# A two-layer hybrid mixer step: the order of the projections in a layer, the filler's rate, and all elementwise work of GpSimd moved to VectorE and ScalarE

## The chip, the cores and the metric

The kernel runs on one core of a Trainium2 chip. The core has TensorE (PE in the profile, with its weight loads as PEld), VectorE (DVE), ScalarE (ACT), GpSimd (POOL) and SyncE (SP). SP and ACT issue the DMA transfers here. The metric is the device time of one execution in microseconds; before the change it is 2315.56 us, the median of three runs (2311.65 to 2316.22).

## The reference

One inference step of a backbone of two layers over 128 context tokens and 512 latent tokens, 640 rows in all, of width 2048. Each layer is one mixer:

```python
def layer_step(x, cvec, p, rope, attend, s0_f, s0_b):
    shift, scale, gate = adaln(cvec, w_ada, b_ada)     # silu(cvec) @ w_ada + b_ada
    h = rms_norm(x, norm_g) * (1.0 + scale) + shift
    aq, ak, av, ag, bq, bff, bfb, bi, bg, cu, cv, cg = split_proj(h @ w_in)
    q, k, v = qkv_heads(aq, ak, av, qg, kg, rope)
    a_out = attend(q, k, v) * jax.nn.silu(ag)
    b_out, s_f, s_b = hgrn_mixer(bq, bff, bfb, bi, bg, lb, hg, s0_f, s0_b)
    c_out = sgu_mixer(cu, cv, cg, lng, lnb, ws, bs)
    y = jnp.concatenate([a_out, b_out, c_out], axis=-1) @ w_out
    return x + gate * y, k, v, s_f, s_b
```

`attend` is windowed attention with 8 query heads and 2 key heads. `hgrn_mixer` is a gated linear recurrence in both directions with 4 heads. `sgu_mixer` normalises `cv`, mixes it over 128 positions in 4 groups and returns `cu * s * silu(cg)`. The forget gates of the recurrence have lower bounds from a softmax over the layers. The outputs are both activations, the new keys and values, and the final states of the recurrence. All is float32.

## The kernel before

**Projections.** Activations are kept transposed, 16 tiles of 128 x 640 per layer. Each float32 operand is split in two parts, `hh` and `hl` for the activations, `wh` and `wl` for the weights (lines 640 and 641: a copy on ACT and a subtraction on DVE), and three products of the parts are summed in PSUM. A projection is either row-major (`rowmajor`, line 663: 512 columns, 15 groups, five PSUM banks) or column-major (`colmajor`, line 680: 128 columns, 4 groups, two banks). There are five PSUM banks for projections and three for all else.

**Order of the work.** The program is written out in full by Python, and a planner places the instructions of each engine by its estimates and by priority, which is the order in which the program names them; the block `hi()` raises it. While a projection's matmuls are written, `tick()` takes one step of the first generator in the list `side` (attention, recurrence, spatial mix), 3 ticks per row-major group and 2 per column-major group, so that their small matmuls stand between the large ones. `flush()` takes all remaining steps at once.

**The filler.** After each group `fill()` (line 328) adds `fill_rate` to a credit and takes one step of the filler for each whole credit. The filler is `ada_steps` (line 290): it sums the modulation of a later use on DVE, one weight slice of 128 x 512 per step (two instructions, lines 300 and 302), 16 slices to a block, and then PE sums the accumulator over the partitions (lines 308 and 319). With two further steps a block has 18. The slices have two buffers and there is one accumulator `aacc`. Layer 0 has 12 blocks: four for its own gate, eight for layer 1's shift and scale. `drain()` takes all steps that are left. In layer 1 four more blocks run at rate 0.5.

**The first layer's start.** x arrives transposed. `first_norm` (line 360) squares it on ACT and sums it over the width on PE with a matrix of ones. `first_round` then computes the first modulation columns and the key projection. `setup` runs ahead of both, `setup2` after `second_round`.

**The rest of a layer.** After the queries and the BI projection (line 326), layer 0 computes CU 1 to 3 and CG 0 and parks them in DRAM (`cud`). Then come four heads of the recurrence (lines 334 to 340; each BFF, BFB, BQ and BG, and the generator `hgrn` of 35 steps joins `side`), the attention gates AG (line 343), CV with the spatial mix `sgu` (line 1164), the remaining AG, and CU and CG (layer 1) or CG 1 to 3 (layer 0). `mul_evac` (line 1202) reads a gate from PSUM, multiplies it into its place and applies the sigmoid; its last product is on POOL for AG and on DVE for CG. `split_mix` (line 1223) splits the 16 tiles of the mixer's output, a quarter of them on POOL, into buffers that the last projection frees one by one. `out_proj` (line 1236) multiplies by the gate and adds x, the addition on POOL for three quarters of the columns; the result of layer 0 is stored by SP. Layer 1 starts with `norm_x`, `scale_x` and `make_h` (line 603), where half of the `hl` are on POOL.

## Time and profile before

| what | us |
|---|---|
| median of 3 runs | 2315.56 |
| lowest and highest | 2311.65 and 2316.22 |
| the profiled execution's own time | 2315.77 |
| its span, first to last instruction | 2313.9 |
| PE busy | 2255.9 |
| DVE busy | 1391.7 |
| ACT busy | 894.0 |
| POOL busy | 120.6 |

The span is what the trace covers; 1.9 us of the execution's own time lie around it. Busy times are sums over one execution. An engine executes its instructions in order, so an instruction that waits holds all that stand behind it on that engine. A row of the profile names an instruction by its line in the kernel, its engine, its operation, and the tiles that it writes and reads (`out<-in`). A wait is put down to what came last before the instruction could start. The granted clock is the share of TensorE's full clock.

### The profile page before, as it was taken

What the parts mean: (1) busy time and instruction counts of PE and PEld (TensorE: products, weight loads), DVE (VectorE), ACT (ScalarE), POOL (GpSimd) and SP (SyncE); (2) the same over time, 40 slices, a digit from 0 to 9 for tenths busy, and PEclk for the clock granted to TensorE, in tenths of its full rate; (3) what the DMA queues carried; (4) which work ended last, traced back from release to release, by engine and by line L of the source; (5) the groups of instructions that cost most, each with busy time, mean ns of one, the idle gap of its engine ahead of it and who ended that gap; (6) DMA issues with size and microseconds to landing.
All of it is one profiled execution on the core that took longest, in us unless ns stands there. A gap on an engine that the chain in (4) does not pass through costs nothing.

```text
span 2313.9 us, 35246 instructions
## 1 busy us (share of the span) xinstructions
PE 2255.9 (97%) x13308; PEld 1958.9 (85%) x13308; DVE 1391.7 (60%) x2686; ACT 894.0 (39%) x2165; POOL 120.6 (5%) x82
## 2 busy tenths in 40 slices
PE   7999999999999999989999999999999999999999
PEld 5766678999999888977787888799999998998887
DVE  3435888877787757665667456855865932434222
ACT  4323334445456522322225234344565542223111
POOL 0000000000000101101112000000000000100110
PEclk9999999999999999999999999999999999999999
DMA  9675633534443445355552221422422423324332
GB/s 329 215 250 184 222 114 91 156 98 125 121 134 98 119 153 155 116 188 161 177 179 82 81 66 50 122 60 75 126 78 77 123 85 92 103 75 150 106 109 82
DMA packets 264878, 296.42 MB, mean 128 GB/s; under 512 B 17378, under 2 KB 166772, under 8 KB 262916
## 3 DMA queue, kind: packets, MB, share of 16 engines
q1 hardware_dynamic: 254368, 271.27, 37.9%
q10 hardware_dynamic: 10340, 22.91, 3.1%
q8 instruction: 104, 1.70, 0.3%
q14 instruction: 66, 0.54, 0.1%
HBM read 280.38 MB, written 13.73 MB: 127 GB/s over the span
## 4 chain that ended last, share of the span: by engine, by line
PE 53%; DVE 6%; DMA 3%; issue 1%; ACT 1%; DVEq 0%; ACTq 0%
PE m L660 21%; PE m L653 9%; PE m L652 9%; PE m L654 9%; DMA wa<-in_w_ada_dram 3%; DVE aacc L302 2%; DVE wl L641 1%; PE s L895 1%; PE s L941 1%; PE s L1108 1%; DVE ev L1261 0%; PE s L319 0%; PE s L1196 0%; PE s L953 0%; PE s L954 0%
## 5 line engine op out<-in xcount | busy, mean ns | idle before, releaser
L641 DVE TENSOR_TENSOR wl<-wr,wh 128x512 fp32r<-128x512 f32 (+1 forms) x535 | 386.9, 725 | 569.2 <-ACT wh L640 562.3
L640 ACT ACTIVATE wh<-wr 128x512 fp32r<-128x512 f32 (+1 forms) x535 | 336.1, 629 | 925.8 <-PE m L654 543.0
L652 PE MATMUL m<-wh,hh 128*128 128x512 f32 x1440 | 571.3, 397 | 9.7 <-DVE mg L1211 6.2
L653 PE MATMUL m<-wl,hh 128*128 128x512 f32 x1440 | 567.1, 394 | 3.5 <-DVE wl L641 3.3
L654 PE MATMUL m<-wh,hl 128*128 128x512 f32 x1440 | 564.9, 393 | 0.0
L660 PE MATMUL m<-hh,wh 128*128 128x384 f32 x2016 | 479.9, 317 | 0.0
L660 PE MATMUL m<-hl,wh 128*128 128x384 f32 x2016 | 465.1, 310 | 0.0
L660 PE MATMUL m<-hh,wl 128*128 128x384 f32 x2016 | 464.8, 310 | 0.0
L302 DVE SCALAR_TENSOR_TENSOR aacc<-wa,s,aacc 128x512 f32<-128x512 f32 x480 | 354.6, 770 | 76.9 <-DMA wa<-in_w_ada_dram 76.2
L652 PEld LDWEIGHTS m<-wh,hh 128*128 128x128 f32 x1440 | 271.9, 189 | 84.6 <-issue 10.3
L653 PEld LDWEIGHTS m<-wl,hh 128*128 128x128 f32 x1440 | 272.1, 189 | 64.2 <-DVE wl L641 7.1
L660 PEld LDWEIGHTS m<-hh,wh 128*128 128x128 f32 x2016 | 311.1, 189 | 13.6 <-issue 12.1
L654 PEld LDWEIGHTS m<-wh,hl 128*128 128x128 f32 x1440 | 271.9, 189 | 58.2 <-issue 2.2
L660 PEld LDWEIGHTS m<-hh,wl 128*128 128x128 f32 x2016 | 310.2, 189 | 1.8 <-issue 1.4
L660 PEld LDWEIGHTS m<-hl,wh 128*128 128x128 f32 x2016 | 310.4, 189 | 1.2 <-issue 0.8
L1094 ACT ACTIVATE mg<-ev,Dt 128x32 f32<-128x32 f32 x480 | 113.0, 309 | 9.4 <-PE s L1108 9.2
L1214 POOL TENSOR_TENSOR mg<-mg,ev 128x640 f32<-128x640 f32 x16 | 26.6, 1663 | 1513.8 <-ACT ev L229 1493.2
L925 ACT ACTIVATE g<-g,st,qs 128x384 f32<-128x384 f32 (+1 forms) x64 | 48.1, 752 | 36.3 <-DVE st L921 36.3
L1263 POOL TENSOR_TENSOR mg<-mg,ev 128x512 f32<-128x512 f32 x30 | 44.4, 1491 | 286.2 <-DVE ev L1261 285.4
L944 ACT ACTIVATE g<-s 128x512 fp32r<-128x512 f32 x56 | 32.5, 596 | 57.5 <-PE s L941 54.1
L945 DVE TENSOR_TENSOR g<-s,g 128x512 fp32r<-128x512 f32 x56 | 38.4, 688 | 23.4 <-ACT g L944 17.0
L1111 DVE COPY_PREDICATED att<-m,s 128x128 f32<-128x128 uint8 x80 | 22.8, 301 | 39.8 <-PE s L1108 39.0
(274 smaller groups left out, 1930.6 us busy)
## 6 DMA issues: line engine op xcount, KB each, us to landing
wr<-in_w_in_dram SPq DMA_DIRECT2D x406, 256.0 KB, 2.9
wa<-in_w_ada_dram SPq DMA_DIRECT2D x278, 256.0 KB, 2.9
wr<-in_w_out_dram SPq DMA_DIRECT2D x128, 256.0 KB, 2.9
wa<-in_w_ada_dram SPq DMA_DIRECT2D x16, 1024.0 KB, 5.3
wa<-in_w_in_dram SPq DMA_DIRECT2D x9, 1024.0 KB, 6.3
wa<-in_w_ada_dram SPq DMA_DIRECT2D x44, 128.0 KB, 3.4
mg<-const_xT_dram SPq DMA_DIRECT2D x4, 1280.0 KB, 5.9
x<-mg SPq DMA_DIRECT2D x20, 256.0 KB, 2.5
```

Source lines behind the costliest of these rows:

```text
L302: nc.vector.scalar_tensor_tensor(acc[:, cd], r, sc, acc[:, cd], op0=ALU.mult, op1=ALU.add)
L640: nc.scalar.activation(wh, raw, AF.Copy)
L641: nc.vector.tensor_tensor(wl, raw, wh.bitcast(F32), op=ALU.subtract)
L652: nc.tensor.matmul(ps, lhsT=hh, rhs=wh[:, 0], start=k == 0, stop=False)
L653: nc.tensor.matmul(ps, lhsT=hh, rhs=wl[:, 0], start=False, stop=False)
L654: nc.tensor.matmul(ps, lhsT=hl, rhs=wh[:, 0], start=False, stop=k == KT - 1)
L660: self.nc.tensor.matmul(ps[hf][:, 0:n], lhsT=w[:, a], rhs=h[:, o:o + n], start=k == 0 and i == 0, stop=k == KT - 1 and i == 2)
L925: nc.scalar.activation(dst[h], src[h], AF.Exp, bias=nmx[:, h:h + 1], scale=rq[:, h:h + 1], accum_out=den[:, h:h + 1])
L944: nc.scalar.activation(pt[0], pb, AF.Copy)
L945: nc.vector.tensor_tensor(pt[1], pb, pt[0].bitcast(F32), op=ALU.subtract)
L1094: nc.scalar.activation(blk[:, 4 * i + q], e[:, q], AF.Copy, scale=dd[:, i, c:c + 1])
L1263: (nc.vector if c == 3 else nc.gpsimd).tensor_tensor(xs, xs, y, op=ALU.add)
```

## The change

1. `first_norm`: the squares are added up on DVE, and PE multiplies the one sum with the matrix of ones (2 products stay of 32).
2. The softmax of the forget bounds (12 operations on DVE, one Exp on ACT) moves from `setup` to the beginning of `setup2`.
3. The division of the attention weights moves from DVE to ACT, and so does the copy of the recurrence's output from PSUM.
4. All of POOL's elementwise work moves to DVE: the `hl` in `make_h` and `split_mix`, the products of the norm in `sgu`, the last product in `mul_evac`, the additions of `out_proj`.
5. The order in a layer: pairs of CU and CG (`cgate`), multiplied and parked in DRAM, three of them ahead of the recurrence's heads in layer 0 and one in layer 1, the others after a head each. Five AG heads follow, then CV, then AG 5 to 7 while the spatial mix runs; these evacuate at once, with another pool of buffers for the sigmoid. After the flush the parked products are loaded and multiplied in, now in both layers.
6. The spatial mix waits ten steps for its matmuls where it waited six.
7. The filler's rate in layer 0 is 0.85 where it was 1.0, and 1.25 in the out-projection.

```diff
     def setup2(self):
...
@@ first_norm
+        tot = self.g()
         for k in range(KT):
-            s = self.g()
+            s = self.g() if k else tot
             nc.scalar.activation(s, xm[k // 4][:, k % 4], AF.Square)
-            for hf, (o, n) in enumerate(HALF):
-                nc.tensor.matmul(b[hf][:, 0:n], lhsT=self.ones, rhs=s[:, o:o + n], start=k == 0, stop=k == KT - 1)
+            if k:
+                nc.vector.tensor_tensor(tot, tot, s, op=ALU.add)
+        for hf, (o, n) in enumerate(HALF):
+            nc.tensor.matmul(b[hf][:, 0:n], lhsT=self.ones, rhs=tot[:, o:o + n], start=True, stop=True)
@@ make_h
-            (nc.gpsimd if kk % 2 else nc.vector).tensor_tensor(hl, h, hh.bitcast(F32), op=ALU.subtract)
+            nc.vector.tensor_tensor(hl, h, hh.bitcast(F32), op=ALU.subtract)
@@ attn
-            nc.vector.tensor_scalar(dst[h], dst[h], den[:, h:h + 1], None, op0=ALU.mult)
+            nc.scalar.activation(dst[h], dst[h], AF.Copy, scale=den[:, h:h + 1])
@@ hgrn
-                nc.vector.tensor_copy(ob[:, j * P:(j + 1) * P], oo[:, 0:P])
+                nc.scalar.activation(ob[:, j * P:(j + 1) * P], oo[:, 0:P], AF.Copy)
@@ sgu
-            (nc.vector if t % 2 else nc.gpsimd).tensor_tensor(v, v, gb, op=ALU.mult)
-            (nc.vector if t % 2 else nc.gpsimd).tensor_tensor(v, v, bb, op=ALU.add)
+            nc.vector.tensor_tensor(v, v, gb, op=ALU.mult)
+            nc.vector.tensor_tensor(v, v, bb, op=ALU.add)
...
-        for _ in range(6):
+        for _ in range(10):
             yield
@@ mul_evac
-    def mul_evac(self, ps, dst, gate, eng=None):
+    def mul_evac(self, ps, dst, gate, eng=None, pool=None):
-            s = self.ev() if gate else None
+            s = (pool or self.ev)() if gate else None
-            (eng or nc.gpsimd).tensor_tensor(dst, dst, s.rearrange("p (t q) -> p t q", q=P), op=ALU.mult)
+            (eng or nc.vector).tensor_tensor(dst, dst, s.rearrange("p (t q) -> p t q", q=P), op=ALU.mult)
@@ split_mix
-            (nc.vector if k % 4 else nc.gpsimd).tensor_tensor(r(hl), src, r(hh.bitcast(F32)), op=ALU.subtract)
+            nc.vector.tensor_tensor(r(hl), src, r(hh.bitcast(F32)), op=ALU.subtract)
@@ out_proj
-                (nc.vector if c == 3 else nc.gpsimd).tensor_tensor(xs, xs, y, op=ALU.add)
+                nc.vector.tensor_tensor(xs, xs, y, op=ALU.add)
@@ begin
-        self.fill_rate = 1.0
+        self.fill_rate = 0.85
@@ layer
-        if l == 0:
-            for h in range(1, 4):
-                self.cu_evac(h, self.colmajor(W, CU + h * P))
...
+        ahead = 3 if l == 0 else 1
+        for h in range(ahead):
+            self.cgate(l, h, W)
         for h in range(NH):
...
             self.side.append(self.hgrn(l, h, es, q))
-        early = 6 if l == 0 else 7
-        for h in range(early):
+            if h < NH - 1 and h + ahead < NH:
+                self.cgate(l, h + ahead, W)
+        for h in range(5):
             self.mul_evac(self.colmajor(W, AG + h * P), self.av_view(h), True)
         self.flush()
         self.sgu_evac(self.rowmajor(W, CV))
         self.side.append(self.sgu(l))
...
+        for h in range(5, 8):
+            self.mul_evac(self.colmajor(W, AG + h * P), self.av_view(h), True, nc.vector, self.g)
+        self.flush()
+        for h in range(NH):
+            u = self.g()
+            nc.scalar.dma_start(u, self.cud[h])
+            nc.vector.tensor_tensor(self.Cm[:, h], self.Cm[:, h], u, op=ALU.mult)
         if l > 0:
             self.drain()
         self.split_mix()
+        if l == 0:
+            self.fill_rate = 1.25
         self.out_proj(l)
         self.drain()
+    def cgate(self, l, h, W):
+        nc = self.nc
+        u = self.g()
+        if l == 0 and h == 0:
+            nc.scalar.dma_start(u, self.cud[0])
+        else:
+            ps = self.colmajor(W, CU + h * P)
+            with self.hi():
+                nc.scalar.activation(u[:, 0:384], ps[0][:, 0:384], AF.Copy)
+                nc.vector.tensor_copy(u[:, 384:640], ps[1][:, 0:256])
+        self.mul_evac(self.colmajor(W, CG + h * P), u.rearrange("p (t q) -> p t q", q=P), True, nc.vector)
+        nc.scalar.dma_start(self.cud[h], u)
```

What layer 0 did after the spatial mix before (AG 6 and 7, the flush, the parked CU multiplied in, CG 1 to 3) and layer 1 (AG 7 ahead of CV, then CU 0 to 3 and CG 0 to 3) goes away.

More of the change, by code (lines that the diff above doesn't have):

```diff
@@ L174, in setup, with setup2 @@
         self.cols = cols
-        l0, l1 = cols[:, 96:104], cols[:, 104:112]
+        self.gs = cst.tile([P, 2, KT, 2], F32, name="gs")
+        self.sh = cst.tile([P, 2, KT, 2], F32, name="sh")
+    def setup2(self):
+        nc, I, C = self.nc, self.I, self.C
+        cst = self.cst
+        l0, l1 = self.cols[:, 96:104], self.cols[:, 104:112]
         lt = self.g(64).rearrange("p (a b) -> p a b", a=8)
@@ L191, in setup @@
         nc.vector.tensor_scalar(self.oml, self.lb, -1.0, 1.0, op0=ALU.mult, op1=ALU.add)
-        self.gs = cst.tile([P, 2, KT, 2], F32, name="gs")
-        self.sh = cst.tile([P, 2, KT, 2], F32, name="sh")
-    def setup2(self):
-        nc, I, C = self.nc, self.I, self.C
-        cst = self.cst
         self.rope = cst.tile([P, 2, 4, 64], F32, name="rope")
@@ L1340, in layer @@
             self.side.append(self.hgrn(l, h, es, q))
-        early = 6 if l == 0 else 7
-        for h in range(early):
+            if h < NH - 1 and h + ahead < NH:
+                self.cgate(l, h + ahead, W)
+        for h in range(5):
             self.mul_evac(self.colmajor(W, AG + h * P), self.av_view(h), True)
         self.flush()
-        if l > 0:
-            self.mul_evac(self.colmajor(W, AG + 7 * P), self.av_view(7), True)
         self.sgu_evac(self.rowmajor(W, CV))
         self.side.append(self.sgu(l))
-        if l == 0:
-            ps = [self.colmajor(W, AG + h * P) for h in (6, 7)]
-            self.flush()
-            for h in (6, 7):
-                self.mul_evac(ps[h - 6], self.av_view(h), True)
-            for h in range(4):
-                u = self.g()
-                nc.scalar.dma_start(u, self.cud[h])
-                nc.vector.tensor_tensor(self.Cm[:, h], self.Cm[:, h], u, op=ALU.mult)
-        else:
-            ps = [self.colmajor(W, CU + h * P) for h in range(2)]
-            self.flush()
-            for h in range(4):
-                self.mul_evac(ps[h] if h < 2 else self.colmajor(W, CU + h * P), self.view(self.Cm, h), False)
-        for h in range(1 - min(l, 1), 4):
-            self.mul_evac(self.colmajor(W, CG + h * P), self.view(self.Cm, h), True, nc.vector)
+        for h in range(5, 8):
[5 more added lines that the diff above has]
+            nc.vector.tensor_tensor(self.Cm[:, h], self.Cm[:, h], u, op=ALU.mult)
         if l > 0:
```

8 lines of the change are left out of this document (removed).

## The prediction

> **What bounds the kernel now.** I read the page first, for the busy shares.
>
> ```profile
> PE 2255.9 (97%) x13308; PEld 1958.9 (85%) x13308; DVE 1391.7 (60%) x2686; ACT 894.0 (39%) x2165; POOL 120.6 (5%) x82
> ```
>
> TensorE (PE) is busy for 2255.9 of 2313.9 us, so the whole prize is the 58 us in which it isn't, plus what the clock loses after such holes. The diff takes almost no matmul away, so the sum below is a sum over holes. The view of waits, PE's own, names them (waiting line, what released it: us in total, times, longest):
>
> ```profile
> PE s L166 <- DVE g L159: 9.4, 1, 9.4
> PE m L652 <- DVE mg L1211: 6.2, 1, 6.2
> PE s L1146 <- DVE g L1140: 6.0, 2, 5.4
> PE s L1196 <- DVE mg L1197: 5.4, 1, 5.4
> PE s L1073 <- ACT g L1069: 4.1, 2, 2.2
> PE m L653 <- DVE wl L641: 3.3, 4, 1.4
> ```
>
> The first is the start, which waits for the first loads. The next three, 6.2, 5.4 and 5.4 us, all lie in the second half of layer 0, and all wait for VectorE (DVE). A table of stretches shows what each costs beside the hole itself (columns: us, PE, PE weight load, DVE, ACT, POOL busy with counts; granted clock; DMA share; GB/s):
>
> ```profile
> 826.00:832.00 6.00, 0.58 (x5) 0.32 (x3) 5.10 (x10) 0.00 (x0) 1.14 (x1) 0.74 0.49 156
> 832.00:836.00 4.00, 4.00 (x18) 3.92 (x18) 3.22 (x9) 0.63 (x1) 0.00 (x0) 0.53 0.31 81
> 917.00:923.00 6.00, 0.59 (x4) 0.40 (x3) 4.33 (x9) 0.00 (x0) 0.00 (x0) 0.84 0.67 202
> 923.00:928.00 5.00, 5.00 (x22) 5.00 (x22) 4.91 (x8) 0.63 (x1) 0.00 (x0) 0.51 0.62 171
> 986.00:993.00 7.00, 0.73 (x2) 0.30 (x2) 2.80 (x6) 2.44 (x5) 1.54 (x1) 0.74 0.53 211
> 993.00:997.00 4.00, 3.98 (x11) 3.17 (x12) 2.99 (x6) 1.02 (x2) 0.00 (x0) 0.60 0.61 188
> ```
>
> PE is busy for 0.6 or 0.7 us in each hole, and then runs for 4 to 5 us at about half clock: 4 x 0.47 = 1.9 us, 5 x 0.49 = 2.4 us, 4 x 0.40 = 1.6 us lost again. The three places cost 5.4 + 1.9 = 7.3, 5.4 + 2.4 = 7.8 and 6.2 + 1.6 = 7.8 us, 23 us together.
>
> Why DVE is late there shows when the filler's accumulation (L302, layer 1's modulation) is cut out by itself (columns: us, DVE busy on that line, clock, DMA share, GB/s):
>
> ```profile
> 801.00:846.00 45.00, 23.53 (x30) 0.92 0.58 183
> 846.00:878.00 32.00, 0.07 (x1) 1.00 0.32 89
> 878.00:930.00 52.00, 22.29 (x30) 0.93 0.58 172
> 930.00:960.00 30.00, 0.00 (x0) 1.00 0.24 70
> 960.00:1017.00 57.00, 23.09 (x30) 0.94 0.60 201
> 1032.00:1076.00 44.00, 22.65 (x30) 1.00 0.61 191
> 1076.00:1102.00 26.00, 0.00 (x0) 1.00 0.32 103
> ```
>
> The filler doesn't run evenly. One block of 16 weight slices is a burst of some 44 us, and then nothing until PE has read the single accumulator. Every hole falls inside a burst; in the quiet stretches the clock is 1.00. So the question for each stage is where the bursts fall after the change.
>
> **The change part by part.** *First norm.* Before, PE adds the squares:
>
> ```profile
> 8.00:36.00 28.00, 22.99 (x102) 15.27 (x102) 5.74 (x24) 15.33 (x28) 0.00 (x0) 1.00 0.98 337
> 11.02 4.48 ACT L366 ACTIVATE g<-mg 128x640 f32<-128x640 f32 x7
> 11.80 19.83 PE L368 MATMUL s<-g,ones 128*128 128x384 f32 x64 [1.72 <-DVE g L184]
> 36.34 0.50 PE L652 MATMUL m<-wh,hh 128*128 128x512 f32 x1 [1.44 <-ACT hh L382]
> L407 SPq DMA_DIRECT2D mg<-const_xT_dram x4: 346/426/432, 1.2 to 7.9; - x4
> DMA to landing us min/median/max: 5.6/5.9/10.9
> 8.42 14.59 SPq L423 DMA_DIRECT2D wa<-in_w_ada_dram  x16
> L1214 DVE TENSOR_TENSOR mg<-mg,ev 128x640 f32<-128x640 f32 x3 | 2.5, 819 | 0.0
> ```
>
> The sum is ready at 11.80 + 19.83 = 31.6 us. Afterwards 15 DVE adds of 0.82 us (the L1214 row is the same shape) make 12.3 us, from about 11.7 to 24.0, since the last of x lands by 7.9 + 10.9 = 18.8 and squares come every 0.64 us (4.48 / 7). One pass over the ones matrix is 19.83 / 16 = 1.2 us, so 25.2 us: 6.4 earlier. The softmax of the forget bounds, whose L184 sits before the first matmul, leaves this stretch too. But the loads set the other pace: DMA is 98% busy at 337 GB/s, and the 16 modulation slices that PE wants next are issued until 8.42 + 14.59 = 23.0. Bounds: 6.4 if PE alone sets the start, 0 if the loads do; I take -4, nearer the upper end, since apart from the 9.4 us at the very start no load is among PE's long waits above.
>
> On this the Trainium skill speaks against the change. TensorE: Matmul & The Clock Gate, Part 1: The HAM clock gate, says that the array runs at half clock by default and after an idle window of about 3.4 us. PE would now idle from some 10 to 24 us, so by the rule the ones pass and the first scale rows run at half clock and the term is nearer -2. The trace agrees as far as it goes: 0.51 to 0.60 after each hole above.
>
> *Burst positions.* One block is 18 filler steps. At rate 1.0 blocks begin every 18 fill calls from the second AQ projection on: calls 126, 144, 162. Counting 15 calls for a row-major and 4 for a column-major projection, that is AG head 4, two thirds through CV, and CG head 2; a burst lasts 12 to 16 calls (44 to 57 us at 3.5). At 0.85 a block takes 21.2 calls: they begin at 127, 148 and 169. After the reordering the heads end at call 122, AG 0 to 4 at 142, CV at 157, AG 5 to 7 at 169.
>
> The last recurrence head ends 35 ticks after its start, at call 139.5, where the burst from 127 has just ended (before: call 132, inside 126 to 138). I take -5 of 7.3; bounds 0 and -7.3.
>
> The spatial mix's matmuls come 12 ticks after CV, with 10 yields for 6, at calls 163 to 165; the burst from 148 is over by 160 to 162 (before: 153 to 155, inside 144 to 156). AG 5 to 7 no longer hold four PSUM banks until the flush, so PE has other work meanwhile. Six of ten norm products move to DVE here, 6 x 0.68 = 4 us, and four more yields give 4 x 1.8 = 7 us of matmul to hide them. I take -6.5 of 7.8; bounds +2 and -7.8.
>
> The split and the first out-projection groups still meet a burst, the one from 169. This hole was made so:
>
> ```profile
> 970.89 1.95 POOL L1232 TENSOR_TENSOR hl<-mg,hh 128x640 fp32r<-128x640 f32 x1 [26.14 <-ACT hh L1231]
> 971.32 2.06 DVE L641 TENSOR_TENSOR wl<-wr,wh 128x512 fp32r<-128x512 f32 x1
> 991.08 1.41 DVE L302 SCALAR_TENSOR_TENSOR aacc<-wa,s,aacc 128x512 f32<-128x512 f32 x2 [4.20 <-DMA wa<-in_w_ada_dram]
> ```
>
> DVE stood for 4.20 us on a filler's load, with the weight split that PE wanted queued behind it. That can recur; what goes is the tail of CG and the GpSimd (POOL) share. I take -3 of 7.8; bounds +4 and -7.8.
>
> *GpSimd to DVE.* A product of 128x640 costs DVE 0.82 us for POOL's 1.6 to 2:
>
> ```profile
> L1214 POOL TENSOR_TENSOR mg<-mg,ev 128x640 f32<-128x640 f32 x16 | 26.6, 1663 | 1513.8 <-ACT ev L229 1493.2
> L1263 POOL TENSOR_TENSOR mg<-mg,ev 128x512 f32<-128x512 f32 x30 | 44.4, 1491 | 286.2 <-DVE ev L1261 285.4
> ```
>
> While POOL ran (970.89 to 972.84) a DVE split that takes 0.69 took 2.06, so 0.82 us of new DVE work replaces up to 1.4 us of delay. I cost the move itself at nothing; without that relief it is 42 x 0.69 (30 adds here and 12 norm products) + 32 x 0.82 = 55 us of DVE time over the kernel, under PE. The stores of layer 0's result sit on SP behind these adds and come sooner by 0.8 us each.
>
> *Out-projection of layer 0.* 169 calls at 0.85 leave 73 of 216 steps, 65 slices, for 60 calls at 1.25.
>
> ```profile
> 983.00:1222.00 239.00, 227.97 (x1010) 185.52 (x1008) 147.03 (x220) 60.33 (x115) 28.74 (x18) 0.99 0.54 176
> L302 DVE SCALAR_TENSOR_TENSOR aacc<-wa,s,aacc 128x512 f32<-128x512 f32 x108 | 81.5, 794 | 31.9 <-DMA wa<-in_w_ada_dram 31.9
> L641 DVE TENSOR_TENSOR wl<-wr,wh 128x512 fp32r<-128x512 f32 x64 | 46.0, 729 | 48.1 <-ACT wh L640 48.0
> ```
>
> A slice (two instructions and its wait) is (81.5 + 31.9) / 54 = 2.1 us. DVE's load becomes 65 x 2.1 + 46 + 40 x 0.69 for products and adds + 8 x 0.82 left of the split = 217 of 239 us, 91%. A block then has 14.4 calls, 57 us, for a burst of 44 to 57. PE lost 3.9 us here to such waits; I take +2; bounds -3.9 and +20.
>
> *The rest.* The division costs ACT 0.71 us for DVE's 0.48:
>
> ```profile
> L599 ACT ACTIVATE mg<-mg,rr 128x512 f32<-128x512 f32 x8 | 5.2, 709 | 0.0
> L930 DVE TENSOR_SCALAR g<-g,st 128x512 f32<-128x512 f32 x32 | 13.7, 482 | 0.2
> ```
>
> ACT is 39% busy and four ticks of matmul follow before PE transposes the result, so 0; if the cover is gone, 20 blocks x 4 x 0.23 = 18 us. But ACT now waits for DVE's reciprocal with later weight splits queued behind, and the same holds for the stores of CU x CG on ACT's queue: 0 to +5. The forget softmax in the second setup puts some 12 tiny DVE operations and one ACT wait ahead of the loads that PE's transposes of the cached keys wait for: +0.5, bounds 0 and +2. In layer 1 the CU/CG pairs between heads remove little, since PE's only holes there are 1.9 and 0.5 us; they hold a buffer each during the recurrence: 0, bounds -2 and +5.
>
> Sum: -4 - 5 - 6.5 - 3 + 2 + 0.5 = -16. From the profiled execution's own 2315.8 us (span 2313.9 and 1.9 around it; the median of the runs is 2315.6) that gives 2299.8, so 2300.
>
> **The rivals.** *All three holes go and the start gains in full:* -6.4 - 7.3 - 7.8 - 7.8 - 2 = -31, 2285. For it: the quiet stretches show clock 1.00. Against: a burst still lies on the split.
>
> *The holes move:* DVE stays at 80 to 90% in layer 0's tail, other in-order DVE work meets the bursts, and only the start is gained: 2312, give or take 4. For it: the tail between CV and the split shrinks from 20 to 12 calls, so DVE has less matmul to hide behind.
>
> *The faster filler becomes the bound, slower than before:* in the out-projection PE itself sums each finished block (L319) at a fixed place in its order. When a burst outlasts the 54 to 57 us that a block has there, PE waits for it, four times. A burst of 57 us already occurred at 960 to 1017, beside the loads of x. At 65 us it is 4 x 9 = 36 us of holes against 14 to 18 us gained: about 2335. It passes the time before from a burst of some 61 us.
>
> *The reordering doesn't do what it says:* the planner places instructions by its own costs, so moved pairs may end where they were. Then about 2315; against it, the three holes before lie at the very calls that were counted above.
>
> **How the numbers follow.** A difference under 0.2%, 4.6 us, can't be told from none. Forecast (2291 to 2308) 0.52; all holes gone (about 2285) 0.16; holes move 0.14; filler bound 0.12; as before 0.06. Faster: 0.52 + 0.16 + half of the third = 0.76; same: the other half and most of the last, 0.11; slower 0.13. The range 2285 to 2317 leaves out the lower part of the second case and the filler bound.
>
> **What would show it.** The ones pass should start near 24 us and the first projection near 32. PE's waits for L1140 and L1197 should shrink below 2 us each with clock 1.00 around them; DVE splits should all take 0.7 us. Filler bursts of 42 to 50 us should lie before the recurrence's and the mix's end. Waits of PE for the accumulator or for L641 of over 10 us after the split would prove the forecast wrong; so would holes in layer 1.

## The result and the profile after

The kernel after takes 2296.81 us (median of four runs, 2296.41 to 2299.35), the kernel before 2315.89 (four runs beside it, 2311.65 to 2317.34): the ratio is 0.9923, with a 95% interval of 0.9908 to 0.9938, some 18 us. Forecast were 2300 with 2285 to 2317. The profiled execution, the slowest of the four, took 2299.35 us with a span of 2297.6 us, 16.3 us shorter than the span before.

The page's busy line of after:

```profile
PE 2241.8 (98%) x13248; PEld 1943.6 (85%) x13248; DVE 1379.9 (60%) x2655; ACT 940.4 (41%) x2289; POOL 0.7 (0%) x8
```

Most lines have moved by three: the weight split, L641 before, is L644. (The lines named above as 326, 334 to 340 and 343 for the BI projection, the heads and AG are 1326, 1334 to 1340 and 1343.) GpSimd keeps only its memsets, and VectorE is busy for 12 us less than the 1391.7 before, though it took over GpSimd's 74 products, adds and splits and the first norm's adds, and gave up the division and the recurrence's copies.

PE's waits of after (waiting line, releaser: us in total, times, longest):

```profile
PE s L371 <- DVE g L369: 14.4, 1, 14.4
...
PE m L656 <- DVE wl L644: 5.5, 5, 2.5
PE s L611 <- issue: 5.3, 1, 5.3
PE s L944 <- ACT g L933: 4.0, 5, 2.3
```

The three waits that the forecast was built on, for L1140, L1197 and L1211, are gone. The 14.4 us are the first norm as designed: PE has nothing to do there until the sum of squares is ready. New are the wait of the out-projection for the weight split, 5.5 us, the longer transition to layer 1 (L611), and the wait for the division, which is now on ACT (L933).

The bursts of the filler in after, as the forecast showed them for before (us, VectorE busy on L302, clock, DMA share, GB/s):

```profile
797.00:848.00 51.00, 21.65 (x30) 1.00 0.50 151
848.00:885.00 37.00, 0.00 (x0) 1.00 0.38 117
885.00:936.00 51.00, 21.35 (x30) 1.00 0.50 147
936.00:971.00 35.00, 0.13 (x1) 1.00 0.44 143
971.00:1022.00 51.00, 21.19 (x30) 0.97 0.65 214
```

The clock is 1.00 through the first two bursts, where it was 0.92 and 0.93. The recurrence's tail (its last transposes from 859 us on) and the spatial mix (its matmuls run from 938.1 to 948.0) lie behind a burst each. The third burst lies on the start of the out-projection, as forecast, and the clock falls there.

The start of after (start us, us, engine, line; the wait in brackets):

```profile
24.42 2.50 PE L371 MATMUL s<-g,ones 128*128 128x384 f32 x4 [14.43 <-DVE g L369]
26.85 3.09 PE L240 MATMUL s<-wa,pad 128*32 128x256 f32 x32
32.57 0.75 PE L655 MATMUL m<-wh,hh 128*128 128x512 f32 x1 [1.44 <-ACT hh L385]
```

The ones pass starts at 24.4 us and the first projection at 32.6, 3.8 us earlier than before.

To see where the time went I compare, in the profiled executions, when the matmuls of the same stage start or end. The table gives the difference to before in us, for after and for the experiments told below.

| kernel | first projection ends | layer 0's out-projection starts | and ends | layer 1's first projection starts | span |
|---|---|---|---|---|---|
| after | -2.3 | -20.3 | -21.1 | -19.2 | -16.3 |
| before, order alone | +0.6 | -13.2 | -12.0 | -12.1 | -13.7 |
| before, filler later | +0.4 | -12.9 | -13.6 | -13.1 | -12.0 |
| before, GpSimd emptied | +0.5 | -10.8 | -17.5 | -17.7 | -18.8 |
| before, GpSimd emptied and filler later | +0.6 | -15.9 | -25.6 | -25.0 | -26.1 |
| after, GpSimd back | -2.2 | -18.3 | -14.6 | -12.6 | -12.9 |
| after, division on VectorE | -1.2 | -21.8 | -25.1 | -23.2 | -25.0 |
| after, bursts moved back | -1.4 | -9.9 | -13.5 | -12.9 | -12.6 |
| after, rate 1.0 | -1.7 | -8.9 | -16.0 | -16.1 | -16.4 |
| after, division on VectorE and PE kept warm | -1.6 | -22.1 | -25.1 | -23.1 | -24.8 |
| the same, and a faster filler | -2.5 | -20.8 | -12.1 | -7.7 | -8.2 |

After gains 2.3 us in the start, 18.0 in the middle of layer 0, 0.8 in its out-projection, and gives 4.8 back behind it. These are single executions, and a difference of 1 to 2 us in one stage can be chance: the first projection starts at 32.6 us in after and at 34.1 in the kernel with only the division changed, whose code is the same up to there.

Two things have to be known to read the table. The out-projection starts at 983.1 us in before, so the hole before the split (PE's wait for L1211, 987 to 993 us) counts in its stretch, not in the middle. And PE sums each of the filler's blocks itself, which takes it 1.7 us; one such sum on the chain of before (start us, us):

```profile
875.82 1.68 PE s L319 x16
```

Before has nine blocks summed ahead of the out-projection and three in it; after, with its two rates, has seven and five. So some 3.4 us of the 18.0 have only moved into the out-projection.

### The profile page after: what moved, and what is told of

Read it like the earlier page. It is cut to its first block, busy times and chain, and to the rows that moved or that the text cites. A ratio compares the mean times of both kernels' runs of the same rounds, so it can differ in the third digit from the quotient of the medians.

```text
span 2297.6 us, 35103 instructions
## 1 busy us (share of the span) xinstructions
PE 2241.8 (98%) x13248; PEld 1943.6 (85%) x13248; DVE 1379.9 (60%) x2655; ACT 940.4 (41%) x2289; POOL 0.7 (0%) x8
## 4 chain that ended last, share of the span: by engine, by line
PE 82%; DVE 7%; DMA 6%; ACT 1%; issue 1%; DVEq 0%; SPq 0%; ACTq 0%
PE m L663 34%; PE m L655 12%; PE m L657 12%; PE m L656 12%; DMA wa<-in_w_ada_dram 5%; DVE aacc L302 2%; PE s L240 2%; PE s L898 2%; DVE wl L644 1%; PE s L944 1%; PE s L1111 1%; PE s L956 1%; PE s L1126 1%; PE s L957 1%; PE s L319 1%
## 5 line engine op out<-in xcount | busy, mean ns | idle before, releaser
L644 DVE TENSOR_TENSOR wl<-wr,wh 128x512 fp32r<-128x512 f32 (+1 forms) x535 | 367.1, 688 | 561.6 <-ACT wh L643 560.4
L302 DVE SCALAR_TENSOR_TENSOR aacc<-wa,s,aacc 128x512 f32<-128x512 f32 x480 | 344.1, 747 | 78.8 <-DMA wa<-in_w_ada_dram 77.4
L944 PE MATMUL s<-misc,g 128*128 128x128 f32 x240 | 45.9, 285 | 4.4 <-ACT g L933 4.0
L933 ACT ACTIVATE g<-g,st 128x384 f32<-128x384 f32 (+2 forms) x80 | 43.8, 605 | 10.9 <-DVE st L931 10.9
L898 PE MATMUL s<-kT,g 128*128 128x256 f32 (+1 forms) x288 | 46.7, 304 | 0.0
L902 DVE CUSTOM_DVE_ANT_0 g<-s,mask 128x384 f32<-128x384 f32 (+1 forms) x64 | 37.9, 622 | 13.3 <-PE s L898 13.1
```

Source lines behind the costliest of these rows:

```text
L302: nc.vector.scalar_tensor_tensor(acc[:, cd], r, sc, acc[:, cd], op0=ALU.mult, op1=ALU.add)
L644: nc.vector.tensor_tensor(wl, raw, wh.bitcast(F32), op=ALU.subtract)
L898: nc.tensor.matmul(so, lhsT=x[:, hs], rhs=y[:, ks], start=i == 0, stop=i == 2, skip_group_check=True)
L944: nc.tensor.transpose(pb[:, h * P:(h + 1) * P], dst[h][:, kb * P:(kb + 1) * P], self.ident)
```

## The experiments

My theory at the start was the forecast's: VectorE is late where one of the filler's bursts falls on a stage that needs it, and the change puts the stages elsewhere. Rivals were that GpSimd slows VectorE, and that the order of the projections does it.

### The filler later, nothing else

```
         self.fill_rate = 1.0
+        self.credit = -12.0
```

> The kernel before with one line more: the filler starts 12 calls later (its credit begins at -12), its rate stays 1.0, and nothing else changes. The blocks then begin at calls 138, 156 and 174, not 126, 144 and 162, so the recurrence's tail (call 132), the spatial mix's matmuls (153 to 155) and the first CG groups lie outside a burst or at its edge. Theory 1, the one of the prediction (the three holes of layer 0 come from where the filler's bursts fall): PE's waits for L1140 and L1197 shrink from 5.4 us each to under 2 us each and the clock around them stays above 0.9; the time falls by 10 to 15 us, to 2301 to 2306. Rival 2 (GpSimd's work slows VectorE and so makes the holes) and rival 3 (the old order of the projections makes them): GpSimd's work and the order are as before, so the waits stay near 5 us and the time within 3 us of the one before.

Measured: 2306.05 us, ratio 0.9954 (0.9941 to 0.9966), -10 us. What its waits have left of the three holes between 820 and 1000 us, and its bursts there:

```profile
PE s L1146 <- DVE g L1140: 2.2, 1, 2.2
PE m L653 <- DVE wl L641: 1.9, 2, 1.0
PE m L652 <- DVE mg L1211: 0.3, 1, 0.3
```

```profile
821.00:851.00 30.00, 0.00 (x0) 0.94 0.34 109
851.00:886.00 35.00, 20.73 (x30) 1.00 0.56 175
886.00:925.00 39.00, 0.44 (x1) 1.00 0.41 127
```

The wait for L1197 isn't in the list any more: the mix, at 908 to 918 us, lies between two bursts, although GpSimd still makes six of its ten products and the order is the old one. The recurrence's tail (826 us) keeps 2.2 of 5.4 us with the burst over since 821. Rivals 2 and 3 expected no change here. The gain is at the lower end of what theory 1 expected, with 2.2 us above its bound for L1140. What those 2.2 us hang on, with no burst there, no run takes apart.

### GpSimd emptied, nothing else

```
-(nc.gpsimd if kk % 2 else nc.vector).tensor_tensor(hl, h, ...)
+nc.vector.tensor_tensor(hl, h, ...)
```

and so at L1181, L1182, L1214, L1232 and L1263.

> The kernel before with only GpSimd's products, adds and splits moved to VectorE; order, filler and first norm as before. Theory 1 (burst positions make the holes): the three holes stay, each 4 to 8 us with its slow clock, and the time changes by -4 to +1 us. Rival 2 (VectorE is slowed by GpSimd): by the duration of each VectorE operation over the median of its own shape while GpSimd runs, 41 us of VectorE time return; if part of that is on the path at the holes, they shrink to about half and the time falls by 8 to 15 us, to 2301 to 2308.

Measured: 2296.92 us, ratio 0.9917 (0.9902 to 0.9932), -19 us. This one part alone brings what the whole change brings; theory 1 had at most 4 us for it, and even the rival's range was passed. Its busy line, its waits and its bursts:

```profile
PE 2255.7 (98%) x13308; PEld 1960.4 (85%) x13308; DVE 1397.9 (61%) x2760; ACT 893.6 (39%) x2165; POOL 0.7 (0%) x8
```

```profile
PE s L1146 <- DVE g L1140: 4.4, 1, 4.4
PE m L652 <- DVE mg L1211: 2.8, 1, 2.8
...
PE s L1196 <- DVE mg L1197: 0.5, 1, 0.5
```

```profile
796.00:845.00 49.00, 21.20 (x30) 0.90 0.55 174
...
874.00:930.00 56.00, 20.78 (x30) 1.00 0.54 162
```

The bursts lie where they lay before. The recurrence's tail (828 us, inside the first) keeps 4.4 us, as theory 1 says. But the mix (910 to 921 us, inside the second) has lost its hole. Two more things show. VectorE took over 74 operations, 55 us by the forecast's estimate, and its busy time rose by only 1397.9 - 1391.7 = 6.2 us. And by the table 6.7 us of the gain (-10.8 to -17.5) come inside the out-projection. There PE waits 10.9 us in all in before (6.2 for L1211, 3.3 for the weight split, 1.4 for two others) and 4.3 in this kernel (2.8 and 1.5): those 6.6 us are nearly all of it.

How GpSimd slows VectorE is seen in the durations of single lines (instructions: ns min/median/max, first and last start, forms), first of before, then of this kernel:

```profile
L641 DVE TENSOR_TENSOR wl<-wr,wh x535: 417/692/2065, 34.4 to 2299.8; 128x512 fp32r<-128x512 f32 x178, 128x256 fp32r<-128x256 f32 x1
L302 DVE SCALAR_TENSOR_TENSOR aacc<-wa,s,aacc x480: 637/747/2061, 207.7 to 1841.2; 128x512 f32<-128x512 f32 x160
L617 DVE TENSOR_SCALAR g<-s,gs,sh x16: 796/804/812, 1229.8 to 1257.2; 128x512 f32<-128x512 f32 x16
```

```profile
L641 DVE TENSOR_TENSOR wl<-wr,wh x535: 419/692/694, 35.0 to 2281.0; 128x512 fp32r<-128x512 f32 x178, 128x256 fp32r<-128x256 f32 x1
L302 DVE SCALAR_TENSOR_TENSOR aacc<-wa,s,aacc x480: 634/745/754, 208.2 to 1823.8; 128x512 f32<-128x512 f32 x160
```

Without GpSimd no split takes longer than 694 ns; with it one took 2065. Summed over the whole trace of before, VectorE's operations that overlap a GpSimd product exceed the median of their own group by 41 us; 19.7 of these are splits and 11.3 the filler's. L617, whose one large input is in PSUM, never exceeds 812 ns, and 11 of its 16 instructions in before ran beside GpSimd. The Trainium skill, SBUF — State Buffer, section "Who interferes with whom", states this: a VectorE instruction with two SBUF inputs contends with a GpSimd instruction that reads SBUF, while one with at most one such input, outside the two-port modes, doesn't. The trace agrees on both halves, with 2065 against 694 ns for L641 and 812 at most for L617. L1180, with one tensor input in SBUF, was slowed too (1.52 us in a row below); whether it ran in a two-port mode the trace doesn't show.

### Only the spatial mix's norm taken from GpSimd

```
-(nc.vector if t % 2 else nc.gpsimd).tensor_tensor(v, v, gb, op=ALU.mult)
+nc.vector.tensor_tensor(v, v, gb, op=ALU.mult)
```

and the same for `bb`; nothing else of GpSimd's work.

> The kernel before with only the spatial mix's norm products (L1181, L1182: six of ten are GpSimd's) moved to VectorE; all else, GpSimd's gate products, splits and residual adds too, as before. In the run with all of GpSimd's work moved, the mix's hole (5.4 us, with its slow clock 7.8) went although the burst lay on it as before, the split's hole halved, and 7 us came in the out-projection. Theory 2a (each hole is made by the GpSimd work of its own stage): the wait for L1197 falls below 1 us, the wait for L1211 before the out-projection stays near 6, and the time falls by 6 to 9 us, to 2307 to 2310. Rival 2b (any part of GpSimd's share slows all of VectorE's stream, so the gain spreads with the total taken away; this is some 8 of 120 us of GpSimd): 0 to -2 us, 2314 to 2316.

Measured: 2309.87 us, ratio 0.9973 (0.9963 to 0.9984), -6 us. The wait for L1197 is gone although the burst lies on it as before (878 to 934 us; mix 914 to 924), and the other holes stand:

```profile
PE s L1146 <- DVE g L1140: 6.1, 2, 5.5
PE m L652 <- DVE mg L1211: 5.7, 1, 5.7
```

So the mix's hole hangs on GpSimd's work of its own stage (2a). The edit took 17 us of work from GpSimd, in both layers (120.6 to 103.4), where the rival counted 8; a share of the 19 us in that proportion would still be under 3. VectorE before and in the run with GpSimd emptied, at the mix (the releaser of the hole is L1197):

```profile
903.15 1.52 DVE L1180 TENSOR_SCALAR ev<-ev,mv 128x512 f32<-128x512 f32 x1
904.59 1.77 DVE L641 TENSOR_TENSOR wl<-wr,wh 128x512 fp32r<-128x512 f32 x1
...
912.78 3.77 DVE L302 SCALAR_TENSOR_TENSOR aacc<-wa,s,aacc 128x512 f32<-128x512 f32 x4 [1.49 <-DMA wa<-in_w_ada_dram]
...
918.63 1.41 DVE L302 SCALAR_TENSOR_TENSOR aacc<-wa,s,aacc 128x512 f32<-128x512 f32 x2 [1.47 <-DMA wa<-in_w_ada_dram]
...
921.88 0.69 DVE L1197 TENSOR_TENSOR mg<-s,g 128x512 f32<-128x512 f32 x1
```

```profile
907.81 1.28 DVE L1182 TENSOR_TENSOR ev<-ev,g 128x512 f32<-128x512 f32 x2
909.02 2.06 DVE L302 SCALAR_TENSOR_TENSOR aacc<-wa,s,aacc 128x512 f32<-128x512 f32 x3
...
911.61 0.68 DVE L1197 TENSOR_TENSOR mg<-s,g 128x512 f32<-128x512 f32 x1
```

Before, the last norm products came from GpSimd at 914 us, and the planner had put eight filler instructions, with two waits for their loads, between the norm and L1197. Without GpSimd three stand there, and none of them waits. Two things differ, then: VectorE's slower operations, and the order that the planner gave it. No run takes them apart, so their shares stay open.

### The order alone

The diff's changes in `layer`, `cgate`, `mul_evac` and the ten yields, at rate 1.0 throughout. GpSimd's work is kept but for the last product of AG 5 to 7, which this part of the diff names for VectorE (6 of 74 operations, 107 us of GpSimd for 121):

```
-        for _ in range(6):
+        for _ in range(10):
...
+            if h < NH - 1 and h + ahead < NH:
+                self.cgate(l, h + ahead, W)
```

> The kernel before with only the reordering: CU/CG pairs between the recurrence's heads, AG 5 to 7 after CV with their sigmoids in another pool of buffers, ten yields ahead of the spatial mix for six. The filler's rate stays 1.0, GpSimd keeps its work, first norm and division are as before. Rival 3 (the order alone removes the holes, by giving PE work where it waited): waits for L1140 and L1197 under 2 us, time down by 12 to 17 us, to 2299 to 2304. Theory 1 (position of the bursts): blocks begin at calls 126, 144 and 162; the recurrence's tail is at 139.5, in the gap between two bursts, so that hole goes; the mix's matmuls at 163 to 165 stand at the start of the third burst and the split at 165 to 180 inside it, so about half of the gain comes, 5 to 10 us: 2306 to 2311.

Measured: 2305.94 us, ratio 0.9956 (0.9944 to 0.9969), -10 us. The tail's matmuls (from 864 us) lie between the bursts of 793 to 842 and 873 to 907, the mix's products on GpSimd end at 934.5, ahead of the next burst from 941, and both waits are gone; before the split 4.9 us for L1211 are left. The time is theory 1's, at the upper end of its 5 to 10 us, but the waits are rival 3's: the mix's matmuls (945 to 955) stand inside the burst of 941 to 1004, where theory 1 expected a hole, and have none. The tail has moved out of a burst. For the mix, either its norm ahead of the burst or the ten yields for six was enough; the run doesn't say which.

### The kernel after with the bursts moved back

```
         self.fill_rate = 0.85
+        self.credit = -5.0
...
-            self.fill_rate = 1.25
+            self.fill_rate = 1.33
```

> The kernel after with only the filler's place moved: its credit begins at -5 and its rate in the out-projection is 1.33 for 1.25, so that bursts lie on the recurrence's tail (call 139.5) and on the spatial mix's matmuls (163 to 165). GpSimd does nothing, as in after. Theory 1 as predicted (a burst on such a place makes a hole of 5 us and a slow clock of 2): holes for L1143 and L1200 return, +10 to +14 us on after, 2307 to 2311. Theory 2 (the hole of the mix needs GpSimd's share as well, that of the recurrence's tail doesn't, as the run with GpSimd's work alone moved showed: 4.4 us there, 0.5 us at the mix): only the recurrence's hole returns, +4 to +8 us: 2301 to 2305. Rival 3 (the order has done it): none returns, within 2 us.

Measured: 2301.82 us, ratio 0.9936 (0.9921 to 0.9952), 3 us slower than after by the ratios, with intervals that overlap. Its waits between 820 and 970 us, and the bursts:

```profile
PE s L1149 <- DVE g L1143: 4.3, 1, 4.3
PE s L1199 <- DVE mg L1200: 0.5, 1, 0.5
```

```profile
821.00:866.00 45.00, 21.45 (x30) 1.00 0.58 178
866.00:915.00 49.00, 0.03 (x1) 0.97 0.30 86
915.00:975.00 60.00, 21.41 (x30) 1.00 0.47 146
```

A burst on the tail (866.9 us) makes its hole again. A burst on the mix (948 to 958) makes only one of 0.5 us, with GpSimd empty. Theory 2 had both right; its price, 4 to 8 us, was a little high for the whole time. By the table this kernel is 10.4 us behind after where the out-projection starts and wins 6.7 back later, 2.6 of it in layer 1, so the 3 us aren't the price of the tail's hole alone.

So the two holes have different conditions. The mix's, in the old order, needs the burst and GpSimd's share together, and taking away either is enough; in the new order it stayed away with a burst on the matmuls and GpSimd's products done ahead of it:

| kernel | mix's matmuls | burst there | GpSimd in its norm | PE waits for the mix's evacuation |
|---|---|---|---|---|
| before | 913 to 931 | 878 to 930 | yes | 5.4 us |
| filler later | 908 to 918 | none | yes | not listed |
| norm products moved | 914 to 924 | 878 to 934 | no | not listed |
| GpSimd emptied | 910 to 921 | 874 to 930 | no | 0.5 us |
| order alone | 945 to 955 | 941 to 1004 | yes, ahead of the burst | not listed |
| after, bursts back | 948 to 958 | 915 to 975 | no | 0.5 us |
| after, rate 1.0 | 949 to 959 | 945 to 1012 | no | not listed |
| after | 938 to 948 | none | no | not listed |

The tail's hole doesn't need GpSimd: with a burst there it measures 4.4 us without GpSimd's work on the old order, and 4.3 in the last run.

### GpSimd emptied and the filler later, on the kernel before

```
         self.fill_rate = 1.0
+        self.credit = -12.0
...
-            (nc.vector if k % 4 else nc.gpsimd).tensor_tensor(r(hl), src, ...)
+            nc.vector.tensor_tensor(r(hl), src, ...)
```

and the other lines of the run with GpSimd emptied.

> The kernel before with all of GpSimd's work moved to VectorE and the filler 12 calls later: the two edits that alone gave -19 and -10 us. If both act on the same holes, they don't add: from the milestones, what the later filler adds is the recurrence tail's hole alone (4.4 us and about 2 of slow clock, which stayed without GpSimd), so 4 to 7 us below the run without GpSimd's work: 2290 to 2293. Rival (the two causes are separate and add): -29 us, 2287 or less. Third (the tail's hole moves to another place, as in the kernel after): 2295 to 2298.

Measured: 2288.76 us, ratio 0.9884 (0.9870 to 0.9897), -27 us, some 8 below GpSimd emptied alone. The time by itself can't choose between 2290 and 2287. The table tells more: up to the out-projection's start the later filler adds 5.1 us (-10.8 to -15.9), where the tail's hole of 4.4 us is gone, as theory 1 said, and where 1.7 us are one block's sum that moved behind that start. The other 3 come inside the out-projection, where no theory had put any: the 2.8 us of waiting for L1211 that GpSimd emptied alone had left there are gone too. Through the tail, the mix and the split PE stands for 0.4 us in all (us, PE, weight load, VectorE, ScalarE, GpSimd busy, clock, DMA share, GB/s):

```profile
720.00:980.00 260.00, 259.60 (x1721) 241.42 (x1720) 198.25 (x362) 115.19 (x297) 0.00 (x0) 1.00 0.49 153
```

This kernel, with the old order, the old norm and the old division, beats both the one before and the one after (0.9870 to 0.9897 against 0.9908 to 0.9938).

### The kernel after with GpSimd's work given back

```
-                nc.vector.tensor_tensor(xs, xs, y, op=ALU.add)
+                (nc.vector if c == 3 else nc.gpsimd).tensor_tensor(xs, xs, y, op=ALU.add)
```

and so at L625, L1184, L1185, L1217 and L1235. GpSimd gets back 68 of its 74 operations (109.7 us for 120.6): the last product of AG 5 to 7 is named for VectorE in after and stays there.

> The kernel after with GpSimd given back what it had before (its share of the splits, of the spatial mix's norm, of the gate products and of the residual adds); order, filler rates, first norm and division as after. Theory 1 alone (only burst positions make holes, and after has them elsewhere): +0 to +4 us on after, 2297 to 2301. Theory 2, as the run with GpSimd's work alone moved suggests (-19 us, of which the spatial mix's hole, half of the split's hole and 7 us in the out-projection of layer 0): VectorE's operations beside GpSimd's grow by some 25 to 40 us in all again, and it costs where VectorE is busiest, in the split and in the out-projection at rate 1.25: +6 to +14 us, 2303 to 2311, with PE's new waits for L1264, L1214 and L644 there and none for the recurrence's tail.

Measured: 2303.30 us, ratio 0.9947 (0.9932 to 0.9961). By the ratios that is 5.5 us slower than after, with intervals that just overlap, as they do for the next kernels set against after: there the trace has to decide. The tail and the mix stay free, as the bursts lie elsewhere. By the table, 2.0 us come before the out-projection and 4.5 in it, and the wait that grows is the one for the weight split:

```profile
PE m L656 <- DVE wl L644: 9.7, 9, 3.4
```

After had 5.5, 5, 2.5 there. The operations beside GpSimd exceed their medians by 29 us again. The time is at the lower edge of theory 2's range, and of the three waits that it named only the one for L644 came. Where layer 1 starts this kernel is 6.6 us behind after; 3.2 of that come back in the BI projection of layer 1, where after loses 2.3 us in one wait for the division and this one 0.4.

### The kernel after at rate 1.0

```
-        self.fill_rate = 0.85
+        self.fill_rate = 1.0
...
-            self.fill_rate = 1.25
```

> The kernel after with the filler's rate at 1.0 through all of layer 0 (no 0.85, no 1.25). Blocks begin at calls 126, 144 and 162. Theory 1: the recurrence's tail (139.5) lies between bursts and stays free; the mix's matmuls (163 to 165) and the split (165 to 180) lie in the third burst: a hole of 3 to 5 us before the out-projection, against which its later part has fewer slices; -2 to +5 us on after, 2295 to 2302. Rival (the two rates are what made the gain of after): +8 us or more. What it tells apart is whether the change of rates was worth anything once GpSimd is empty.

Measured: 2298.57 us, ratio 0.9926 (0.9911 to 0.9940). The new rates are worth nothing that can be told from none, but two large amounts cancel in that. This kernel starts its out-projection 11.4 us later than after (3.4 of them the two blocks' sums, which stand ahead of it again) and wins as much back: in the out-projection 7.1 for after's 0.8, although a wait of 3.6 us for the split stands at 999 us, 2 us in the transition to layer 1, and some 3 in layer 1.

### The kernel after with the division on VectorE

```
-            nc.scalar.activation(dst[h], dst[h], AF.Copy, scale=den[:, h:h + 1])
+            nc.vector.tensor_scalar(dst[h], dst[h], den[:, h:h + 1], None, op0=ALU.mult)
```

> The kernel after with only the division of the attention's output back on VectorE. In the trace after PE waits 4.0 us for L933 on ScalarE (before: 1.3 us), 2.3 us of it in one hole in layer 1 that is followed by 3.4 us at half clock. Theory (ScalarE's later finish is on the path, the prediction's cover of four ticks doesn't always hold): -2 to -4 us on after, 2293 to 2295. Rival (the cover holds and what is lost there comes from elsewhere): within 1 us of after.

Measured: 2291.77 us, ratio 0.9900 (0.9884 to 0.9917), some 5 us faster than after by the ratios. The hole in layer 1, in after, PE and VectorE:

```profile
1469.79 0.69 PE L944 MATMUL s<-misc,g 128*128 128x128 f32 x2 [2.29 <-ACT g L933]
```

```profile
1467.59 0.75 DVE L302 SCALAR_TENSOR_TENSOR aacc<-wa,s,aacc 128x512 f32<-128x512 f32 x1 [0.94 <-DMA wa<-in_w_ada_dram]
...
1468.86 0.17 DVE L931 RECIPROCAL st<-st 128x4 f32<-128x4 f32 x1
```

The reciprocal stood behind a filler instruction that waited 0.94 us for its load and behind a weight split, then ACT began the division, and PE stood for 2.3 us and ran on at a clock of 0.50 for 3.3 us more. With the division on VectorE, PE's waits at this line sum to 1.9 us for 4.0. That accounts for layer 1: by the starts and ends of its stages, 3.4 us come in the BI projection and 1.0 in the recurrence. The price hangs on what the planner put ahead of the reciprocal: with the division on ScalarE too, the kernels with the bursts back, with GpSimd's work back and at rate 1.0 wait 0.5, 0.4 and 1.3 us at this place for after's 2.3.

In layer 0 this profiled execution gains 3.7 us between BI and CV, after a start that was up to 2 us later, and 2.8 in the first chunk of the out-projection, where no division runs. In that chunk PE waits for the weight split three times for 3.9 us, in after four times for 5.0, and the clock is 0.97 for 0.95; the runs leave open why. The two profiled executions are 8.5 us apart and the medians 5, so a part of this is chance.

### The first norm alone, and PE kept warm in it

The first run is before with the diff's changes in `first_norm` and the forget softmax in `setup2`:

```
+            if k:
+                nc.vector.tensor_tensor(tot, tot, s, op=ALU.add)
+        for hf, (o, n) in enumerate(HALF):
+            nc.tensor.matmul(b[hf][:, 0:n], lhsT=self.ones, rhs=tot[:, o:o + n], start=True, stop=True)
```

> The kernel before with only the first norm changed (VectorE adds the squares, PE makes one pass of the ones matrix) and the forget softmax moved into the second setup. The trace after showed the ones pass at 24.4 us and the first projection 3.8 us earlier, its end 2.4 us earlier. Theory 1 (this start is a gain of its own and the layers behind it follow it): time down by 2 to 4 us, to 2312 to 2314, with the first projection 3 to 4.5 us earlier. Rival (the loads set the start's end, so that the earlier norm is eaten up by waits for the modulation's slices): under 1 us of gain.

Measured: 2316.20 us, ratio 1.0003 (0.9994 to 1.0012). The first projection started 3.1 us earlier and ended 1.8 earlier, the out-projection of layer 0 started at the same time as before, and at the end nothing was left. The second run is the kernel after with the division on VectorE and

```
+            if k >= 4:
+                nc.tensor.matmul(b[0][:, 0:384], lhsT=self.ones, rhs=s[:, 0:384], start=True, stop=True)
```

> The kernel after with the division back on VectorE and with twelve products of the ones matrix with a square of x (384 columns each, into the bank that the ones pass then overwrites) during the first norm, so that PE doesn't stand for 14.4 us before the ones pass. The added products do no part of the computation. Against the run with only the division back (2291.8). Theory (the idle PE runs at half clock afterwards: ones pass 2.50 us for 1.24, scale rows 3.09 for 1.93): the ones pass and the scale rows return to about 1.3 and 1.9 us, the first projection starts 1.5 to 2.5 us earlier, and the time falls by 1 to 2.5 us, 2289 to 2291. Rival (the loads or VectorE set the first projection's pace, so what is won at its start is lost in it): within 0.7 us.

Measured: 2295.06 us, ratio 0.9905 (0.9892 to 0.9919), no different from the run without it. Its start:

```profile
25.27 1.34 PE L373 MATMUL s<-g,ones 128*128 128x384 f32 x4 [1.57 <-DVE g L369]
26.55 1.93 PE L240 MATMUL s<-wa,pad 128*32 128x256 f32 x32
```

The rows are back at 1.34 for 2.50 and 1.93 for 3.09 us, and the first projection starts at 31.55 us, 2.5 us earlier than in the run beside it (34.06). It ends only 0.4 us earlier, at 128.2 for 128.6. The first steps of the projection, here and in the run beside it (us, PE, weight load, VectorE, ScalarE, GpSimd busy, clock, DMA share, GB/s):

```profile
31.50:38.00 6.50, 6.45 (x15) 4.84 (x15) 3.43 (x5) 1.51 (x3) 0.00 (x0) 0.52 0.92 278
34.00:38.00 4.00, 3.94 (x11) 3.08 (x11) 3.43 (x5) 1.53 (x4) 0.00 (x0) 0.58 0.88 261
```

At these clocks the first stretch loses 6.5 x 0.48 = 3.1 us and the second 4.0 x 0.42 = 1.7. The half-speed rows were real and idling was their cause, as the forecast took from the Trainium skill (TensorE: Matmul & The Clock Gate, Part 1: The HAM clock gate); only their durations show it, for the clock column reads 1.00 from 24.4 to 30 us in after. But removing them buys nothing: the first projection gives 2.1 us back, some 1.4 of them by a longer stretch at half clock at its own start.

### A faster filler in the out-projection

As the last, with

```
-            self.fill_rate = 1.25
+            self.fill_rate = 1.4
```

> As the run before it (division back, PE kept warm), with the filler's rate in the out-projection 1.4 for 1.25, so that its last slices end some 8 calls (30 us) before layer 0 ends and not inside the norm between the layers, where PE stood for 5.3 and 2.5 us and then ran at half clock until 14 us after the first of them had begun. Theory (the filler's last slices and the layer's last adds, queued on VectorE ahead of the norm, make the longer hole): the first of the two waits falls to about 1.7 us as in the runs at rate 1.0, and the time by 2 to 4 us. Rival (the denser filler makes new waits of the same size for the split L644 at the out-projection's start): within 1 us.

Measured: 2306.78 us, ratio 0.9963 (0.9949 to 0.9976), 13 us slower than at 1.25. Both theories missed it. By the table 11.7 us of it come in the out-projection and 2.4 in the transition.

```profile
PE s L613 <- issue: 7.6, 1, 7.6
PE s L319 <- DVE aacc L302: 5.1, 2, 4.9
```

The second line is PE waiting for the filler's sum at its fixed place, the forecast's third rival, which at 1.25 doesn't show; after it PE ran at a clock of 0.50 (1021.9 to 1027 us). Layer 0's last block did end earlier (1172 us for 1177 in the run with only the division back), but then the planner pulled more of layer 1's own first block into the gap: 26 instructions of L302 between 1180 and 1230 us for 6, and the wait of the transition grew from 5.3 to 7.6 us.

## Why the forecast came out right, step by step

The sum was -16 and the profiled execution shows -16.4, the medians some -18. That they fit so closely is partly luck: the start gave 1.7 us less than its term, the middle of layer 0 more than its terms, and what lies behind layer 0 cost 4.8 us that the sum had at nothing. These errors cancel.

*First norm, -4.* Measured 2.3 us at the end of the first projection, near the -2 that the forecast gave for half clock after the idle stretch, and nothing at the end when it was made alone. For the whole time the lower bound was the right one: of what the start wins, the projection loses a part again. The runs don't separate the loads from the projection's own first steps at half clock, where the run with PE kept warm lost some 1.4 of the 2.1 us that it gave back.

*Recurrence tail, -5 of 7.3.* Right in cause: the burst from call 127 had ended, and putting a burst back brought 4.3 us of hole back. The whole hole went, so it was a little low.

*Spatial mix, -6.5 of 7.8.* The gain came, but not by the step's reason alone. A burst on the mix makes no hole once GpSimd is out of its norm, and made none in the new order with GpSimd's products done ahead of it. After has all of these cures and needs no single one of them: with a burst put back (0.5 us left) or with GpSimd put back the hole stays away. With the softmax's +0.5 the tail and the mix gave -11.0; the middle of layer 0 shows -18.0, without the moved sums some -14.6, which is about the whole of both holes (7.3 + 7.8 = 15.1).

*Split, -3 of 7.8, and out-projection, +2.* These share one stretch, and together gave -1; measured -0.8. That the two agree is luck: the two moved sums, 3.4 us, stand in the measured number and in neither term, so what the terms speak of gained some 4.2. The wait for L1211 went, and PE's waits for the split rose from 3.3 to 5.5 us, as the step allowed ("that can recur"). With GpSimd's work given back the stretch is 3.7 us longer than before, about what the moved sums take; GpSimd's relief, costed at zero, is what after has on top. The bursts there took 37 to 51 us, far from the 61 of the third rival.

*GpSimd to DVE, 0.* This is the step that failed: "I cost the move itself at nothing". It named the relief, 1.4 us per product, and let it cancel the 55 us of added work under PE. VectorE's busy time did nearly cancel, +6.2 us. But the relief falls where VectorE is late, and so it reaches PE: -19 us when made alone on before, some 5.5 us lost when nearly all of it was undone on after. The step weighed sums of VectorE time where it should have asked in which stage each lengthened operation stood.

*The rest and layer 1, 0 with +5 for ACT's division.* Measured at that bound: undoing the division gives about 5 us. The forecast named the mechanism, ACT waiting for the reciprocal, and took the wrong end. The transition to layer 1, for which there was no term, cost 1.9 us more (-21.1 to -19.2). In after two instructions of layer 1's first filler block stand on VectorE ahead of the norm in this gap. From the last matmul of the out-projection to the first of layer 1 the gap is 9.3 or 9.4 us in the six kernels with no filler instruction in it or in the 12 us before, 10.0 in the three with three of them just before it, 11.4 or 11.5 in the four with two inside and more before, and 13.7 in the last run. That fits, but no run changed it alone.

*The signs.* The ones pass (24.4 us), the first projection (32.6), the waits for L1140 and L1197 and the splits (697 ns at most in after) came as the forecast said. But it also said that holes in layer 1 would prove it wrong, and there after has a new one of 2.3 us at the division, beside the longer wait of 5.3 us in the transition.

So the rest of the change brings nothing on top of an empty GpSimd that these runs can tell from none (0.9923 for 0.9917): what order and rates gain at the recurrence's tail, the division and the transition take back. The rivals "filler becomes the bound" and "the reordering does nothing" are out; the order alone gave 10 us.

## What to carry to other kernels

A hole can need two conditions at once, and then two cures each look like the cause; undo each alone, from before and from after, ahead of crediting either. Work on an engine that looks idle isn't free if it lengthens another engine's operations: look at the maximum of a line's durations beside its median, and ask in which stage the long ones stand. A change of many parts that wins can hold a part that loses: here one line, the division, held some 5 us, and only in the schedule that the other parts gave. Before a gain is put down to a stage, ask whether work was won there or only moved to the next one: here 3.4 us of sums had moved.

## What the hardware showed that was not expected

A split or an accumulation on VectorE took up to 2.06 us for 0.69 or 0.75 beside GpSimd, and with GpSimd empty VectorE did 74 more operations in 6.2 us more busy time.

A short hole was enough for the half clock: in after PE stood for 2.29 us at 1467.5 and the granted clock was 0.50 for the next 3.3 us:

```profile
1467.50:1469.80 2.30, 0.01 (x2) 0.01 (x1) 2.21 (x5) 0.68 (x2) 0.00 (x0) 0.97 0.48 146
1469.80:1473.10 3.30, 3.30 (x13) 2.64 (x13) 1.28 (x2) 1.46 (x3) 0.00 (x0) 0.50 0.75 215
```
